# Gate and up projections in seven block products for eight, and the hidden layer in three parts

## The chip, the core and the metric

The kernel runs on one core of one Trainium2 chip. The metric is the device time of one execution in microseconds (us); lower is better. PE is TensorE, DVE VectorE, ACT ScalarE, POOL GpSimd, and SP the engine whose queue issues most transfers.

## What is computed

A trunk of two layers over 512 frames of width 1024. Each layer is a feed-forward block (FFN), an attention mixer, and a second FFN; so there are four FFNs, and they are what the change touches. Everything is float32. Cut to what matters:

```python
def _swiglu(u, w_gate, w_up, w_down):          # w_gate, w_up 1024 x 2816, w_down 2816 x 1024
    return (jax.nn.silu(u @ w_gate) * (u @ w_up)) @ w_down
...
mod = (cond @ ada_w[i] + ada_b[i]).reshape(c.shape[0], N_MOD, D_MODEL)[:, :, None, :]
sh1, sc1, g1, sh2, sc2, g2, sh3, sc3, g3 = [mod[:, j] for j in range(N_MOD)]
u = _rmsnorm(h, norm_g[i, 0]) * (1 + sc1) + sh1
h = h + MACARON_WEIGHT * g1 * _swiglu(u, ffn_w_gate[i, 0], ffn_w_up[i, 0], ffn_w_down[i, 0])
```

After the first FFN comes the mixer with g2, then the second FFN with sh3, sc3 and g3.

## The kernel before

Activations lie transposed: features on the 128 partitions, the 512 frames along the row. A weight chunk of 128x1024 is loaded as `raw` (`wload`), and `wsplit` makes a rounded part `wh` (a copy on ACT) and the rest `wl` (a subtraction on DVE). `mm3` multiplies in three matmuls, wh by the activation's rounded part, wh by its rest, and wl by the rounded part. So every product waits for ACT and then for DVE on its weights, and each matmul loads a 128x128 block and streams the frames past it.

`ffn` makes the 22 tiles of the hidden layer one after the other (`unit`): 24 matmuls of 512 frames for gate into a `pj` bank, 24 for up into an `s` bank, then `gated` (Silu on ACT, product on DVE, split into hid tiles by both). The first tiles of each FFN stand apart, since they run in halves of 256 frames while the norm before them ends, or, in the first FFN, as x arrives. When all 22 are there, `back_proj` makes the eight output tiles (k = 0 to 7) of 66 matmuls each from three weight chunks, and adds each to h (`Back.tile`), the last tile in halves.

The modulation `mod` is the largest other load: 144 chunks of 512 KB (`ada_chunk`), each multiplied with `cond` and summed on DVE. They stand in the list `pending`. `background(n)` issues the next n of them, and each multiply is placed behind the last instruction noted in `mark`, on DVE's queue. `need` issues as many as it takes until a gate's columns are there. All of this runs from in-order queues, one an engine. [...]

## Time and profile before

| | |
|---|---|
| median of 3 runs | 2013.37 us (2010.99 to 2013.88) |
| the profiled execution's own time | 2006.17 us |
| its span, first to last instruction | 2004.4 us |
| PE busy | 1956.1 us, 98% of the span |
| DVE busy | 1094.6 us, 55% |
| ACT busy | 744.7 us, 37% |
| POOL busy | 120.4 us, 6% |

Shares are means over the whole span. The stages follow each other: the start and the first FFN up to about 388 us, the first mixer up to 704, an FFN up to 1070, an FFN up to 1426, the second mixer up to 1626, and the last FFN. A profiled execution and a median of other executions need not agree to the microsecond; here they lie 7.2 us apart.

### The profile page before, as it was taken

How to read it: one execution, taken by the hardware profiler on the slowest of the kernel's cores; microseconds unless marked ns; L12 is line 12 of the kernel's file. 1: busy time of each engine (PE TensorE's matmuls, PEld its weight loads, DVE VectorE, ACT ScalarE, POOL GpSimd, SP SyncE). 2: the span in 40 equal slices, each digit the busy share in tenths (PEclk: the TensorE clock that was granted, in tenths of full speed). 3: DMA queues.
4: the chain of work that ended last, by engine and by line, in shares of the span. 5: the costliest groups of instructions: out<-in, count | busy, mean ns of one | idle time of the engine just before them, and what ended most of it. 6: DMA issues, size and time to landing. Idle time of an engine off the chain costs nothing.

```text
span 2004.4 us, 25366 instructions
## 1 busy us (share of the span) xinstructions
PE 1956.1 (98%) x9988; PEld 1652.8 (82%) x9988; DVE 1094.6 (55%) x1893; ACT 744.7 (37%) x1232; POOL 120.4 (6%) x116
## 2 busy tenths in 40 slices
PE   7999999999989999999999999999999999999997
PEld 4888888987878888888889888888988898888886
DVE  7466673479946577777336433323586573333234
ACT  6322222246667442222224233222357543232221
POOL 0000000045553000000000000000000000000000
PEclk9999999999999999999999999999999999999998
DMA  9467773232222238887432333233232023322331
GB/s 334 135 228 241 236 234 105 92 107 67 85 79 80 85 121 270 280 274 248 117 97 85 107 99 95 92 98 97 71 99 71 23 94 109 103 95 95 95 97 61
DMA packets 78412, 260.53 MB, mean 130 GB/s; under 512 B 9426, under 2 KB 12498, under 8 KB 78292
## 3 DMA queue, kind: packets, MB, share of 16 engines
q1 hardware_dynamic: 75892, 254.65, 39.5%
q0 software_dynamic: 1664, 3.28, 0.7%
q8 instruction: 78, 1.28, 0.3%
q10 hardware_dynamic: 736, 0.98, 0.2%
q14 instruction: 42, 0.34, 0.1%
HBM read 249.17 MB, written 2.10 MB: 125 GB/s over the span
## 4 chain that ended last, share of the span: by engine, by line
PE 83%; DVE 10%; ACT 3%; DMA 2%; issue 1%; POOL 1%; SPq 0%; DVEq 0%; ACTq 0%; POOLq 0%
PE pj L299 18%; PE pj L301 18%; PE pj L300 18%; PE s L301 9%; PE s L300 9%; PE s L299 9%; DVE hid L978 1%; DVE m L977 1%; DVE wl L266 1%; DVE hid L767 1%; DVE hid L350 1%; DVE sm L699 1%; PE aux L718 1%; ACT wide L707 1%; ACT wh L265 1%
## 5 line engine op out<-in xcount | busy, mean ns | idle before, releaser
L265 ACT ACTIVATE wh<-raw 128x1024 fp32r<-128x1024 f32 (+1 forms) x331 | 340.8, 1030 | 899.6 <-PE pj L300 561.9
L266 DVE TENSOR_TENSOR wl<-raw,wh 128x1024 fp32r<-128x1024 f32 (+2 forms) x308 | 364.6, 1184 | 417.5 <-ACT wh L265 417.0
L299 PE MATMUL pj<-u,wh 128*128 128x512 f32 (+1 forms) x1035 | 391.1, 379 | 2.0 <-ACT u L349 0.9
L301 PE MATMUL pj<-u,wl 128*128 128x512 f32 (+1 forms) x1035 | 382.5, 370 | 0.7 <-DVE wl L266 0.5
L300 PE MATMUL pj<-u,wh 128*128 128x512 f32 (+1 forms) x1035 | 381.4, 370 | 0.8 <-DVE u L350 0.8
L299 PE MATMUL pj<-hid,wh 128*128 128x512 f32 (+1 forms) x876 | 319.5, 365 | 0.2 <-DVE h L441 0.2
L300 PE MATMUL pj<-hid,wh 128*128 128x512 f32 (+1 forms) x876 | 317.2, 362 | 0.0
L301 PE MATMUL pj<-hid,wl 128*128 128x512 f32 (+1 forms) x876 | 317.2, 362 | 0.0
L301 PE MATMUL s<-u,wl 128*128 128x512 f32 (+1 forms) x841 | 311.3, 370 | 0.0
L300 PE MATMUL s<-u,wh 128*128 128x512 f32 (+1 forms) x841 | 310.8, 370 | 0.0
L299 PE MATMUL s<-u,wh 128*128 128x512 f32 (+1 forms) x841 | 310.6, 370 | 0.0
L299 PEld LDWEIGHTS pj<-u,wh 128*128 128x128 f32 x1035 | 196.3, 190 | 35.6 <-issue 3.1
L301 PEld LDWEIGHTS pj<-u,wl 128*128 128x128 f32 x1035 | 195.5, 189 | 34.4 <-DVE wl L266 1.5
L300 PEld LDWEIGHTS pj<-u,wh 128*128 128x128 f32 x1035 | 195.6, 189 | 31.2 <-DVE u L350 1.9
L186 DVE SCALAR_TENSOR_TENSOR wide<-wide,cond 128x1024 f32<-128x1024 f32 x133 | 161.3, 1223 | 73.4 <-DMA wide<-in_ada 73.2
L299 PEld LDWEIGHTS pj<-hid,wh 128*128 128x128 f32 x876 | 165.5, 189 | 25.8 <-DVE hid L770 0.4
L301 PEld LDWEIGHTS pj<-hid,wl 128*128 128x128 f32 x876 | 165.3, 189 | 25.4
L300 PEld LDWEIGHTS pj<-hid,wh 128*128 128x128 f32 x876 | 165.4, 189 | 24.9
L301 PEld LDWEIGHTS s<-u,wl 128*128 128x128 f32 x841 | 158.8, 189 | 26.8
L300 PEld LDWEIGHTS s<-u,wh 128*128 128x128 f32 x841 | 158.6, 189 | 26.5
L299 PEld LDWEIGHTS s<-u,wh 128*128 128x128 f32 x841 | 158.5, 189 | 26.0
L557 DVE TENSOR_TENSOR t<-t,s 128x512 f32<-128x512 f32 (+1 forms) x93 | 60.5, 651 | 162.8 <-PE s L301 159.5
(214 smaller groups left out, 1920.2 us busy)
## 6 DMA issues: line engine op xcount, KB each, us to landing
raw<-in_wgu SPq DMA_DIRECT2D x176, 512.0 KB, 3.5
wide<-in_ada SPq DMA_DIRECT2D x133, 512.0 KB, 4.4
raw<-in_wd SPq DMA_DIRECT2D x64, 512.0 KB, 3.5
raw<-in_wd SPq DMA_DIRECT2D x32, 384.0 KB, 3.1
raw<-in_hin SPq DMA_DIRECT2D x19, 512.0 KB, 3.5
h<-in_ada SPq DMA_DIRECT2D x11, 512.0 KB, 7.1
raw<-in_hv SPq DMA_DIRECT2D x8, 512.0 KB, 3.5
raw<-in_hout SPq DMA_DIRECT2D x8, 512.0 KB, 3.6
```

The source lines that it names most:

```text
L186: V.scalar_tensor_tensor(raw, raw, 1.0, cond[0], op0=ALU.mult, op1=ALU.mult, accum_out=mod[l][:, j, k:k + 1])
L265: S.activation(wh[:, :n], raw[:, :n], AF.Copy)
L266: (by or V).tensor_tensor(wl[:, :n], raw[:, :n], wh[:, :n].bitcast(F32), op=ALU.subtract)
L299: PE.matmul(ps, ah, bh, start=start, stop=False)
L300: PE.matmul(ps, ah, bl, start=False, stop=False)
L301: last_mm[0] = PE.matmul(ps, al, bh, start=False, stop=stop).ins
L350: return V.tensor_tensor(ol, raw, oh.bitcast(F32), op=ALU.subtract)
L557: V.tensor_tensor(sg[:, :w], sg[:, :w], pu[:, :w], op=ALU.mult)
L699: V.tensor_reduce(nmx, ps[:, :n], axis=AX.X, op=ALU.max, negate=True)
L707: S.activation(pr[qt], pr[qt], AF.Copy, scale=rinv[:, qt:qt + 1])
L718: last_mm[0] = PE.transpose(ps[:, c:c + P], pr[qt][:, kt * P:(kt + 1) * P], ident).ins
L767: V.tensor_tensor(ol, ps, oh.bitcast(F32), op=ALU.subtract)
```

## The change

**Products.** Two hidden tiles are made at once (`pair`). For gate and for up, the 2x2 blocks of weights (two chunks of 128 inputs by two tiles) and of activations (two chunks by two halves of 256 frames) are multiplied in seven block products (`pair_products`): for each of four pairs of input chunks, seven times three matmuls of 256 frames, into four banks. Three of the seven weight blocks are sums, made by three POOL subtractions in `weight_sums`; ACT and DVE then split 896 columns. The activations' sums are made once an FFN (`input_sums`), by POOL, and split. Four DVE additions put the tiles together from the banks.

**Parts.** The hidden layer is made in three parts of 6, 8 and 8 tiles, and after each part the down projection of that part is added to h for all eight output tiles. The gate's columns g are so wanted after the first part. In the last part three output tiles run in halves, where one did.

**Modulation.** The rate of `background` is one chunk a pair (it was 2 to 4 a tile) and two an output tile in the first two parts. The chunks land in the `raw` buffers, four now for two, which the weights use too, and no longer in the two `wide` ones. `g3` of the first layer is loaded in the second FFN.

The diff, cut to its core:

```diff
-NRAW = 2
+NRAW = 4
...
     def ada_chunk(l, j, k, raw=None):
-        raw = wide_tile()[:, :D] if raw is None else raw
+        raw = raw_tile() if raw is None else raw
...
+    def input_sums(t1, t2):
+        lo, hi = slice(0, HALF), slice(HALF, T)
+        G.tensor_tensor(t1[:, lo], t1[:, hi], t1[:, lo], op=ALU.subtract)
+        G.tensor_tensor(t1[:, hi], t1[:, hi], t2[:, hi], op=ALU.add)
+        G.tensor_tensor(t2[:, hi], t2[:, hi], t1[:, lo], op=ALU.add)
+        G.tensor_tensor(t2[:, lo], t2[:, lo], t2[:, hi], op=ALU.subtract)
...
+    def weight_sums(ap):
+        raw = raw_tile()
+        nc.sync.dma_start(raw[:, :512], ap)
+        r = raw.rearrange("p (s c) -> p s c", s=8)
+        G.tensor_tensor(r[:, 4:6], r[:, 0:1].to_broadcast([P, 2, P]), r[:, 1:4:2], op=ALU.subtract)
+        G.tensor_tensor(r[:, 6], r[:, 3], r[:, 4], op=ALU.subtract)
+        G.tensor_tensor(r[:, 7], r[:, 2], r[:, 6], op=ALU.subtract)
...
+        S.activation(wh[:, :896], raw[:, P:], AF.Copy)
+        V.tensor_tensor(wl[:, :896], raw[:, P:], wh[:, :896].bitcast(F32), op=ALU.subtract)
+        return wh, wl
...
+    def pair_products(src, u, sums):
+        banks[0] += 1
+        b = [pj_ps(), s_ps(), aux_ps(), s_ps() if banks[0] % 2 else aux_ps()]
...
+                mm3(o, wh[:, sl], wl[:, sl], *x, q == 0 and n < 4, q == KD // 2 - 1 and n in (0, 4, 5, 6))
+        r = wide_tile().rearrange("p (s c) -> p s c", s=5)
+        S.activation(r[:, 3], b[0][:, lo], AF.Copy)
...
+        V.tensor_tensor(r[:, 0:5:4], r[:, 3:4].to_broadcast([P, 2, HALF]), two(b[1]), op=ALU.add)
+        V.tensor_tensor(r[:, 1:3], r[:, 4:5].to_broadcast([P, 2, HALF]), two(b[2]), op=ALU.add)
+        V.tensor_tensor(r[:, 3], r[:, 2], b[2][:, lo], op=ALU.add)
+        V.tensor_tensor(r[:, 1:3], r[:, 1:3], two(b[3]), op=ALU.add)
...
+    PARTS = ((0, 6), (6, 14), (14, 22))
...
+        def pair(j):
+            g = pair_products(lambda q: d["wgs"][l, f, j // 2, 0, q], u, sums)
+            S.activation(g, g, AF.Silu)
+            p = pair_products(lambda q: d["wgs"][l, f, j // 2, 1, q], u, sums)
+            V.tensor_tensor(p, p, g, op=ALU.mult)
+            for i in range(2):
+                hidden.append((hid_tile(), hid_tile()))
+                mark[0] = split(*hidden[-1], p[:, i * T:(i + 1) * T]).ins
+            background(rate[0])
...
-        for j in range(j0, NF):
-            unit(j, *load(j), 0, T)
-            background(rate)
...
+        for p0, p1 in PARTS:
+            for j in range(max(j0, p0), p1, 2):
+                pair(j)
...
+            g = gate()
+            if p1 < NF:
+                for k in range(KD):
+                    ps = pj_ps()
+                    run_tile(ps, down(k), act, 0, T)
+                    mark[0] = V.scalar_tensor_tensor(h[:, k], ps, g[:, k:k + 1], h[:, k],
+                                                     op0=ALU.mult, op1=ALU.add).ins
+                    background(rate[1])
+            else:
+                back_proj(g, down, act, nxt, 3)
...
-    pending.extend(ada_work(0, [("g", 0), ("n", 1), ("g", 1), ("n", 2), ("g", 2)]))
+    pending.extend(ada_work(0, [("g", 0), ("n", 1), ("g", 1), ("n", 2)]))
```

In the rows of order below, raw, wh and wl are weights, and `raw<-raw,cond` into mod is a modulation chunk's multiply.

**Place 1, DVE in the down projection of the first FFN.** Before, between two additions to h from pj banks:

```order
L266 TENSOR_TENSOR wl_2347<-raw_2344,wh_2346 128x1024
L366 TENSOR_TENSOR t_2077<-t_2077,t_2251 128x512
L266 TENSOR_TENSOR wl_2353<-raw_2350,wh_2352 128x1024
L266 TENSOR_TENSOR wl_2359<-raw_2356,wh_2358 128x768
L441 SCALAR_TENSOR_TENSOR h<-pj_2254,g_0_997,h 128x512
L266 TENSOR_TENSOR wl_2436<-raw_2433,wh_2435 128x1024
L366 TENSOR_TENSOR t_2077<-t_2077,t_2340 128x512
L266 TENSOR_TENSOR wl_2442<-raw_2439,wh_2441 128x1024
L266 TENSOR_TENSOR wl_2448<-raw_2445,wh_2447 128x768
```

After the change, in the first part's down projection (768 columns are six tiles' weights):

```order
L269 TENSOR_TENSOR wl_977<-raw_974,wh_976 128x768
L269 TENSOR_TENSOR wl_1009<-raw_1006,wh_1008 128x768
L691 SCALAR_TENSOR_TENSOR h<-pj_973,g_0_970,h 128x512
L189 SCALAR_TENSOR_TENSOR raw_999,mod_92<-raw_999,cond_94 128x1024
L189 SCALAR_TENSOR_TENSOR raw_1002,mod_92<-raw_1002,cond_94 128x1024
L691 SCALAR_TENSOR_TENSOR h<-pj_1005,g_0_970,h 128x512
L189 SCALAR_TENSOR_TENSOR raw_1031,mod_92<-raw_1031,cond_94 128x1024
L189 SCALAR_TENSOR_TENSOR raw_1034,mod_92<-raw_1034,cond_94 128x1024
L269 TENSOR_TENSOR wl_1041<-raw_1038,wh_1040 128x768
L269 TENSOR_TENSOR wl_1073<-raw_1070,wh_1072 128x768
L691 SCALAR_TENSOR_TENSOR h<-pj_1037,g_0_970,h 128x512
```

Each addition to h is now followed by two modulation multiplies, and the weights of the next two output tiles stand behind two such groups.

**Place 2, DVE where the first FFN's gate columns g_0 are formed.** Before, in the middle of the hidden tiles:

```order
L350 TENSOR_TENSOR hid_991<-t_987,hid_990 128x512
L186 SCALAR_TENSOR_TENSOR wide_994,mod_92<-wide_994,cond_94 128x1024
L186 SCALAR_TENSOR_TENSOR wide_1000,mod_92<-wide_1000,cond_94 128x1024
L208 TENSOR_TENSOR g_0_997<-mod_92,vec 128x8
L210 TENSOR_SCALAR g_0_997<-g_0_997 128x8
L266 TENSOR_TENSOR wl_1165<-raw_1162,wh_1164 128x1024
L186 SCALAR_TENSOR_TENSOR wide_1003,mod_92<-wide_1003,cond_94 128x1024
L557 TENSOR_TENSOR t_1068<-t_1068,s_1043 128x512
L266 TENSOR_TENSOR wl_1171<-raw_1168,wh_1170 128x1024
```

After the change, between the first part's last pair (its last hid split is the first row) and its down projection:

```order
L353 TENSOR_TENSOR hid_935<-wide_923,hid_934 128x512
L189 SCALAR_TENSOR_TENSOR raw_946,mod_92<-raw_946,cond_94 128x1024
L189 SCALAR_TENSOR_TENSOR raw_949,mod_92<-raw_949,cond_94 128x1024
L189 SCALAR_TENSOR_TENSOR raw_952,mod_92<-raw_952,cond_94 128x1024
L189 SCALAR_TENSOR_TENSOR raw_955,mod_92<-raw_955,cond_94 128x1024
L189 SCALAR_TENSOR_TENSOR raw_958,mod_92<-raw_958,cond_94 128x1024
L189 SCALAR_TENSOR_TENSOR raw_961,mod_92<-raw_961,cond_94 128x1024
L189 SCALAR_TENSOR_TENSOR raw_964,mod_92<-raw_964,cond_94 128x1024
L189 SCALAR_TENSOR_TENSOR raw_967,mod_92<-raw_967,cond_94 128x1024
L211 TENSOR_TENSOR g_0_970<-mod_92,vec 128x8
L213 TENSOR_SCALAR g_0_970<-g_0_970 128x8
L269 TENSOR_TENSOR wl_977<-raw_974,wh_976 128x768
```

The multiplies that stood one to three a tile now stand in one run of eight, ahead of the first weights of the down projection.

**Place 3, DVE among the hidden tiles.** Before, one tile of the first FFN:

```order
L557 TENSOR_TENSOR t_1224<-t_1224,s_1199 128x512
L266 TENSOR_TENSOR wl_1327<-raw_1324,wh_1326 128x1024
L350 TENSOR_TENSOR hid_1228<-t_1224,hid_1227 128x512
L186 SCALAR_TENSOR_TENSOR wide_1231,mod_92<-wide_1231,cond_94 128x1024
L186 SCALAR_TENSOR_TENSOR wide_1234,mod_92<-wide_1234,cond_94 128x1024
L266 TENSOR_TENSOR wl_1404<-raw_1401,wh_1403 128x1024
L186 SCALAR_TENSOR_TENSOR wide_1237,mod_92<-wide_1237,cond_94 128x1024
```

After the change, half of a pair's cycle, from the product of gate and up to the end of the next gate's recombination:

```order
L645 TENSOR_TENSOR wide_1489<-wide_1489,wide_1358 128x1024
L580 TENSOR_TENSOR wl_1648<-raw_1642,wh_1647 128x896
L353 TENSOR_TENSOR hid_1497<-wide_1489,hid_1496 128x512
L580 TENSOR_TENSOR wl_1678<-raw_1672,wh_1677 128x896
L353 TENSOR_TENSOR hid_1501<-wide_1489,hid_1500 128x512
L189 SCALAR_TENSOR_TENSOR raw_1504,mod_92<-raw_1504,cond_94 128x1024
L580 TENSOR_TENSOR wl_1708<-raw_1702,wh_1707 128x896
L609 TENSOR_TENSOR wide_1631<-wide_1631,s_1508 128x2x256
L610 TENSOR_TENSOR wide_1631<-wide_1631,aux_1509 128x512
L580 TENSOR_TENSOR wl_1738<-raw_1732,wh_1737 128x896
L611 TENSOR_TENSOR wide_1631<-wide_1631,aux_1509 128x256
L612 TENSOR_TENSOR wide_1631<-wide_1631,s_1510 128x512
```

The weights' splits are 896 wide, four a product, and four additions that read PSUM banks stand between them.

## Rows read from the trace of the kernel before

**Rows 1.** The page: busy time of each engine, and the chain that ended last.

```profile
PE 1956.1 (98%) x9988; PEld 1652.8 (82%) x9988; DVE 1094.6 (55%) x1893; ACT 744.7 (37%) x1232; POOL 120.4 (6%) x116
...
PE 83%; DVE 10%; ACT 3%; DMA 2%; issue 1%; POOL 1%; SPq 0%; DVEq 0%; ACTq 0%; POOLq 0%
```

**Rows 2.** Windows: a down projection, 18 hidden tiles; columns as its head says.

```profile
core 0: us, PE busy (x) PEld busy (x) DVE busy (x) ACT busy (x) POOL busy (x), PEclk, DMA share, GB/s
...
263.10:388.00 124.90, 124.71 (x611) 105.72 (x610) 60.34 (x95) 31.17 (x38) 1.04 (x2) 1.00 0.44 138
...
1110.40:1306.00 195.60, 195.60 (x865) 161.97 (x864) 74.05 (x84) 58.23 (x76) 0.00 (x0) 1.00 0.31 98
```

**Rows 3.** Timeline of PE (start, duration in us): first and last of 20 matmuls.

```profile
699.93 0.28 PE L300 MATMUL pj<-hid,wh 128*128 128x256 f32 x1
...
702.20 0.28 PE L301 MATMUL pj<-hid,wl 128*128 128x256 f32 x1
```

**Rows 4.** Groups by line and shape on DVE: busy us, mean ns, idle before.

```profile
L266 DVE TENSOR_TENSOR wl<-raw,wh 128x1024 fp32r<-128x1024 f32 x268 | 328.0, 1224 | 306.9 <-ACT wh L265 306.4
L186 DVE SCALAR_TENSOR_TENSOR wide<-wide,cond 128x1024 f32<-128x1024 f32 x133 | 161.3, 1223 | 73.4 <-DMA wide<-in_ada 73.2
...
L557 DVE TENSOR_TENSOR t<-t,s 128x512 f32<-128x512 f32 x81 | 55.5, 686 | 159.5 <-PE s L301 159.5
...
L266 DVE TENSOR_TENSOR wl<-raw,wh 128x768 fp32r<-128x768 f32 x36 | 34.5, 957 | 110.6 <-ACT wh L265 110.6
L441 DVE SCALAR_TENSOR_TENSOR h<-pj,g,h 128x512 f32<-128x512 f32 x34 | 25.5, 750 | 66.6 <-PE pj L301 66.6
...
L186 DVE DVE_READ_ACCUMULATOR wide<-wide,cond 128x1 f32 x133 | 10.9, 82 | 0.0
```

**Rows 5.** Groups by line and shape on ACT.

```profile
L265 ACT ACTIVATE wh<-raw 128x1024 fp32r<-128x1024 f32 x291 | 308.3, 1059 | 769.5 <-PE pj L300 440.6 <-issue 195.1 <-PE s L300 60.6
...
L265 ACT ACTIVATE wh<-raw 128x768 fp32r<-128x768 f32 x36 | 30.5, 846 | 127.9 <-PE pj L300 119.5 <-PE pj L301 3.9 <-DMA raw<-in_wd 2.2
```

**Rows 6.** DMA issues: count, KB each, median us from issue to landing.

```profile
wide<-in_ada SPq DMA_DIRECT2D x133, 512.0 KB, 4.4
...
raw<-in_wd SPq DMA_DIRECT2D x32, 384.0 KB, 3.1
...
raw<-in_uqr SPq DMA_DIRECT2D x4, 192.0 KB, 2.4
```

**Rows 7.** Timeline of PE around a wait in the first mixer.

```profile
423.71 0.38 PE L299 MATMUL pj<-wh,u 128*128 128x256 f32 x1 [0.85 <-ACT wh L265]
426.71 0.39 PE L300 MATMUL pj<-wl,u 128*128 128x256 f32 x1 [2.62 <-POOL wl L266]
...
427.68 0.41 PE L299 MATMUL pj<-wh,u 128*128 128x256 f32 x1
...
430.03 0.41 PE L301 MATMUL pj<-wh,u 128*128 128x256 f32 x1
```

**Rows 8.** Windows around the same wait, columns as in rows 2.

```profile
417.00:427.00 10.00, 6.54 (x38) 5.25 (x37) 9.23 (x9) 3.81 (x6) 6.11 (x4) 1.00 0.57 156
427.00:430.50 3.50, 3.50 (x19) 3.50 (x19) 3.40 (x5) 2.14 (x4) 3.45 (x4) 0.51 0.48 150
```

**Rows 9.** Timeline of POOL, subtractions and products in the first mixer.

```profile
417.79 2.38 POOL L266 TENSOR_TENSOR wl<-raw,wh 128x1024 fp32r<-128x1024 f32 x1
...
609.36 1.28 POOL L658 TENSOR_TENSOR hid<-hid,hid 128x512 f32<-128x512 f32 x1
...
616.66 1.29 POOL L658 TENSOR_TENSOR hid<-hid,hid 128x512 f32<-128x512 f32 x1
```

**Rows 10.** Timeline of DVE at the same times.

```profile
417.47 3.25 DVE L350 TENSOR_TENSOR hid<-hid,hid 64x512 fp32r<-64x512 f32 x1
...
610.28 1.45 DVE L266 TENSOR_TENSOR wl<-raw,wh 128x1024 fp32r<-128x1024 f32 x1 [1.49 <-ACT wh L265]
...
616.80 0.69 DVE L350 TENSOR_TENSOR hid<-aux,hid 128x512 fp32r<-128x512 f32 x1
```

More of the change, by code (lines that the diff above doesn't have):

```diff
@@ L181, with raw_tile @@
     mark = [None]
+    def raw_tile():
+        return wp.tile([P, 1024], F32, tag="raw", name=nm("raw"), bufs=NRAW)
     def ada_chunk(l, j, k, raw=None):
-        raw = wide_tile()[:, :D] if raw is None else raw
+        raw = raw_tile() if raw is None else raw
         nc.sync.dma_start(raw, d["ada"][l, j * KD + k])
@@ L246, in wload @@
     def wload(ap, n):
-        raw = wp.tile([P, 1024], F32, tag="raw", name=nm("raw"), bufs=NRAW)
+        raw = raw_tile()
         nc.sync.dma_start(raw[:, :n], ap)
@@ L540, in first_products @@
             mm3(ps, wh[:, sl], wl[:, sl], *u[k], k == 0, k == KD - 1)
-    def ffn(l, f, u, gate, nxt, feed=None, rate=2, after=None):
+    HALF = T // 2
+    def input_sums(t1, t2):
[4 more added lines that the diff above has]
+        G.tensor_tensor(t2[:, lo], t2[:, lo], t2[:, hi], op=ALU.subtract)
+        out = []
+        for t in (t1, t2):
+            o = hid_tile(), hid_tile()
+            split(*o, t)
+            out += [tuple(x[:, c] for x in o) for c in (lo, hi)]
+        return [out[0], out[3], out[1], out[2]]
@@ new lines, with two @@
+    banks = [0]
+    def pair_products(src, u, sums):
+        banks[0] += 1
+        b = [pj_ps(), s_ps(), aux_ps(), s_ps() if banks[0] % 2 else aux_ps()]
+        lo, hi = slice(0, HALF), slice(HALF, T)
+        for q in range(KD // 2):
+            wh, wl = weight_sums(src(q))
+            b1, b2 = u[2 * q], u[2 * q + 1]
+            t1, t2, t3, t4 = sums[q]
+            for n, (o, w, x) in enumerate((
+                    (b[0][:, lo], 0, [v[:, lo] for v in b1]),
+                    (b[1][:, lo], 1, [v[:, lo] for v in b2]),
+                    (b[2][:, lo], 4, t1),
+                    (b[3][:, lo], 6, [v[:, hi] for v in b2]),
+                    (b[1][:, hi], 5, t2),
+                    (b[2][:, hi], 3, t3),
+                    (b[3][:, hi], 2, t4))):
+                sl = slice(w * P, (w + 1) * P)
+                mm3(o, wh[:, sl], wl[:, sl], *x, q == 0 and n < 4, q == KD // 2 - 1 and n in (0, 4, 5, 6))
+        r = wide_tile().rearrange("p (s c) -> p s c", s=5)
+        S.activation(r[:, 3], b[0][:, lo], AF.Copy)
+        def two(x):
+            return x.rearrange("p (s c) -> p s c", s=2)
+        V.tensor_tensor(r[:, 0:5:4], r[:, 3:4].to_broadcast([P, 2, HALF]), two(b[1]), op=ALU.add)
+        V.tensor_tensor(r[:, 1:3], r[:, 4:5].to_broadcast([P, 2, HALF]), two(b[2]), op=ALU.add)
+        V.tensor_tensor(r[:, 3], r[:, 2], b[2][:, lo], op=ALU.add)
+        V.tensor_tensor(r[:, 1:3], r[:, 1:3], two(b[3]), op=ALU.add)
+        return r.rearrange("p s c -> p (s c)")[:, :2 * T]
@@ L543, in ffn @@
+    PARTS = ((0, 6), (6, 14), (14, 22))
+    def ffn(l, f, u, sums, gate, nxt, feed=None, rate=(2, 2), after=None):
         hidden = []
@@ L577, in ffn @@
                 gated(j, *pss[j], 0, T)
+            unit(j0, *load(j0), 0, T)
+            j0 = 4
         else:
@@ L588, in ffn, with down, u_next @@
                     gated(j, *pss, c0, c1)
-        for j in range(j0, NF):
-            unit(j, *load(j), 0, T)
-            background(rate)
-            if after is not None and j == after[0]:
-                after[1]()
-        def down(k):
-            out = []
-            for c, (k0, k1) in enumerate(((0, 8), (8, 16), (16, 22))):
-                wh, wl = wchunk(d["wd"][l, f, k][:, k0 * P:k1 * P], (k1 - k0) * P)
-                out.append((wh, wl, k1 - k0))
-            return out
-        back_proj(gate(), down, hidden, nxt, 1)
-    def u_next(l, sub):
+        for p0, p1 in PARTS:
+            for j in range(max(j0, p0), p1, 2):
+                pair(j)
+            if after is not None and p1 == NF:
+                after()
+            act = hidden[p0:p1]
+            def down(k):
+                return [(*wchunk(d["wd"][l, f, k][:, p0 * P:p1 * P], (p1 - p0) * P), p1 - p0)]
+            g = gate()
[8 more added lines that the diff above has]
+                back_proj(g, down, act, nxt, 3)
+    def u_next(l, sub, keep=False):
         outs = [(u_tile(), u_tile()) for _ in range(KD)]
+        kept, sums = [], []
         def nxt(acc, c0, c1):
@@ L618, in two @@
                     rb = spread(dg[0], c1 - c0)
-                apply(h_tiles(), rb, c0, c1, acol[l, sub], bcol[l, sub], outs)
+                if keep and not kept:
+                    kept.extend(hid_tile(F32) for _ in range(KD))
+                apply(h_tiles(), rb, c0, c1, acol[l, sub], bcol[l, sub], outs, kept)
+                if keep and c1 == T:
+                    for q in range(KD // 2):
+                        for k in (2 * q, 2 * q + 1):
+                            G.tensor_scalar(kept[k], kept[k], bcol[l, sub][:, k:k + 1], None, op0=ALU.add)
+                        sums.append(input_sums(kept[2 * q], kept[2 * q + 1]))
             later(HOLD1, one)
             later(HOLD2, two)
-        return outs, nxt
+        return (outs, sums), nxt
     def rope_tables(fcol, scol):
@@ L1292, in final @@
                     nc.sync.dma_start(d["out"][:, 4 * g:4 * g + 4, c0:c1], o)
-            ffn(1, 1, u, need(gcol, (1, 2)), final)
+            ffn(1, 1, *x, need(gcol, (1, 2)), final)
 def _consts():
```

46 lines of the change are left out of this document (29 added, 17 removed).

## The prediction

> **What bounds the kernel now.** I read the page first: PE is busy for 98% of the span, and 83% of the chain that ended last is PE's; DVE, at 55%, has 10% of it [rows 1]. The windows say the same stage by stage: through 18 hidden tiles, and in a down projection, PE is busy for practically all of the time [rows 2]. So before, whatever the other engines do is hidden. The change takes work from PE and gives DVE and POOL more, so two questions decide: what PE's part is worth, and where PE must now wait for a queue that had slack.
>
> **Columns.** 18 tiles took 195.6 us [rows 2], 10.87 a tile, 21.73 a pair. In 256-frame form 19 steps from the first to the last of 20 matmuls took 2.27 us [rows 3], 0.1195 each. A pair is now 2 x 84 of them, 20.07. Seven products for eight would be 12.5% less, but the narrow form costs more a column, and 1.66 us a pair (7.6%) is left. There are 39 pairs (9 in the first FFN, where four tiles stand apart, 10 in the others): **-65 us**. Two more output tiles an FFN in halves cost 0.6 us each time, which I put with the small things.
>
> **Down projection with modulation chunks.** Place 1 of the order is the largest term. Per output tile DVE has an addition to h, 0.75, and two chunk multiplies of 1.223 + 0.082 [rows 4]. An addition waits for PE's last matmul of its tile, and the multiplies are placed behind it, so none can run ahead. The weights of tiles 2 and 3 stand behind the second group. So PE ends tile 1, and only then DVE does an addition (0.75), two multiplies (2.61) and the first split (0.96 for 768 columns) [rows 4]: 4.3, with gaps 4.5; PE, which has no other work in its row, waits. With 1024 columns the split is 1.22, the wait 4.7. I checked that it is not the load: that chunk can be issued when the first group's first multiply has freed a buffer, 2.05 us after tile 0's end; 3.1 landing [rows 6], 0.85 on ACT [rows 5] and the split make 7.0, and the queue gets there at 8.6 (one tile of 18 matmuls is 4.1). This comes three times a part, and a fourth time before the next part's first product. The order shows it in five parts: two each in the first and second FFN, the first in the third. 5 x 4 x 4.6 = **+92**. It could be nothing only if the multiplies left the queue between; the order excludes that.
>
> **The clock.** Before, PE had been idle for most of 3 us when, just after it took up work at 426.71, the 256-frame matmuls took 11 steps in 2.35 us, 0.214 each [rows 7], and the granted clock of that stretch was 0.51, the lower of the two levels (1.2 of 2.4 GHz), after 1.00 [rows 8]. Some 17 matmuls at 0.094 more are 1.6 us lost. The 20 waits above are longer than that one. Bounds 0 and 1.7 a wait; I take the row it is nearest to, 1.6: **+32**.
>
> **The gate after the first part.** Place 2. PE needs the hid splits of the last pair and the first down weights. From the last product's end: a copy on ACT and hand-overs 0.55, four additions (three at 0.69; one of 256 columns at about 0.42, by the splits' slope of 1.04 ns a column) 2.5 [rows 4], the product of 1024 columns 1.22, two splits 2.1: 6.5. Then eight multiplies follow. Four buffers are full: 5.2, until 11.7. Each of the others waits for a buffer from the multiply four before it and for a landing, 4.4 by the chunks' row [rows 6]: the last ends at about 17.3. The down weights take a buffer of the fifth, 3.1 and 0.85 more, and split at 18.3. PE idles for all of it. The second FFN has seven multiplies there: 17.3. **+36**, and 3 for the clock, which goes into the small things. In the third FFN the gate is there long before.
>
> **The other ends of parts** would cost 6.5 minus six tiles (4.1) each, but PE's row lets tile 1 begin in between: 0.3 to 1.5 each, some 10. The second FFN's last part has three chunks after an addition, ahead of tile 1's weights: 6, and two waits of 2: 10. **+20.**
>
> **Inside the pairs.** Per pair DVE has eight splits of 896 columns (between 0.957 and 1.224 [rows 4]: 1.09), eight additions (5.0), a product (1.22), two hid splits (1.37), gaps (0.6): 16.9, and 18.2 with a chunk; PE's 20.07 covers it. POOL's forms are not in the trace; from 1.28 at 512 columns and 2.38 at 1024 [rows 9], 256 is 0.73 and 128 is 0.46: 1.65 a weight block, 13.2 a pair, which is covered too. But the two are not independent. At 417 a DVE split of two SBUF operands lasted 3.25 for 0.69 and ended when POOL's subtraction did and half a microsecond more; at 610 one of 1024 columns lasted 1.45 for 1.22, again behind POOL; at 616.8 a split that reads PSUM (aux) lasted 0.69 right through POOL's work [rows 9, 10]. So each split, product and chunk multiply can wait for the POOL instruction that runs, up to 0.73, and the additions from PSUM do not. A chunk also holds one of four `raw` buffers over its pair, and a weight block then waits for the third before it: landing some 2.6 (between 2.4 for 192 KB and 3.1 for 384 [rows 6]), POOL 1.65, ACT 0.95, DVE 1.09 and hand-overs, 6.8. Closed around DVE's row (third place), that is 20.4 a pair without any wait for POOL. With nine DVE instructions on this loop, each waiting 0.17 on average, and POOL's own waits, 22.3: 2.2 over PE. Bounds: 0 (all waits covered), and 5.7 (every such DVE instruction and every POOL one apart: 12.6 + 13.2 = 25.8 minus 20.07). I take 2.2, nearer the low end since POOL's instructions are short: 17 pairs, **+37**. The 22 pairs without a chunk have four buffers and 3.2 us of DVE slack: 0.3 each, **+7**; uncovered it would be 4.4.
>
> The Trainium skill, SBUF — State Buffer, section Who interferes with whom, says that a DVE instruction with two SBUF inputs contends with a GpSimd instruction that reads SBUF, as an exclusive lock for the whole instruction. The three places above agree with it; taken as if both engines always met, it gives the upper bound, the second rival.
>
> **Small things**: input sums on POOL and DVE at each FFN's start (at most three us each, mostly ahead of need), halves, the clock at the gate's two waits. **+8.**
>
> **Sum.** -65 + 92 + 32 + 36 + 20 + 37 + 7 + 8 = +167. On the profiled execution's 2006.2 that is 2173; the median lies 7.2 above that execution, so 2180.
>
> **Rivals.**
> *Cheap waits.* POOL and DVE interleave without loss, and PE is back at full clock at once: without 37, 7 and 32 the sum is +91: 2104. For it: POOL's instructions are short, and DVE has slack on average. Against: a row that shows the clock fall after a shorter wait.
> *The port is the bound.* DVE's and POOL's instructions exclude each other throughout: 17 x 5.7 + 22 x 4.4 = 194 in place of 44: 2330. For it: the long waits at 417. Against: at 610 the split behind POOL took 0.14 less than alone, and the additions from PSUM leave POOL room.
> *Not slower.* The chunk multiplies cost PE nothing, because DVE gets to the weights behind them before PE needs them, as it did before. All of the large terms are waits behind such multiplies: 92, their clock 32, the gate's 36, 10 at the second FFN's last part and 37 in the pairs, 207 together; without them 1973. It decides at a fifth of that: below 40 in all the kernel is not slower, which is a wait of about 1.2 us, clock and all, where I have 6.2. For it: DVE is busy for 55% only, and 133 such multiplies cost PE nothing before. Against: a queue in the order printed cannot pass an addition that waits for PE.
> *The change does nothing to PE*: if the narrow matmuls took half of 0.227 they would give 2.7 a pair, and if 0.13 nothing; the twenty steps speak against both.
>
> **How the numbers follow.** Forecast (2140 to 2230) 0.62; cheap waits (2085 to 2140) 0.15; port (2230 to 2350) 0.16; not slower 0.07, of it 0.03 within 0.2% of 2013 (what a measurement of this kernel can tell from no change) and 0.04 faster. The range leaves the ends of the two outer cases out: 2090 to 2270. Slower 0.93.
>
> **What would show it.** PE's busy share falls from 98% to about 88%. A pair without a chunk takes 20.1 to 20.5 between its Silus, one with a chunk about 22. In the first FFN's first down projection PE shows waits of some 4.5 us for wl at every second output tile, and one of about 18 ahead of it, with the clock at the lower level after them. Weight splits of 896 columns last over 1.09 on average. It is wrong if those waits are not there, or if the pairs take 24 and more.

## The result and the profile after

The changed kernel takes **2271.07 us** (median of 4 runs, 2266.89 to 2274.52), the kernel before 2013.62 beside it: **1.128** times as long, with an interval of 1.1258 to 1.1302. The forecast was 2180, in a range of 2090 to 2270. The direction was right, the size 91 us too small, and the time lies just above the range. The profiled execution took 2274.52 us over a span of 2272.7; against the 2006.2 of before that is +268, which is what the parts below are summed to (the medians lie 257 apart).

The page, busy time of each engine and the chain that ended last, as in [rows 1]:

```profile
PE 2010.7 (88%) x12820; PEld 1794.3 (79%) x12820; DVE 1565.1 (69%) x2434; ACT 917.6 (40%) x1467; POOL 1023.1 (45%) x1140
...
PE 41%; POOL 22%; DVE 19%; DMA 6%; issue 6%; ACT 5%; POOLq 0%; DVEq 0%; SPq 0%; ACTq 0%
```

PE's share fell to 88%, as forecast, and more than half of the chain is no longer PE's; of the others POOL has most, 22%. What PE waited for, in us, times and the longest:

```profile
PE pj L302 <- ACT wh L268: 73.9, 25, 17.3
PE pj L304 <- DVE wl L580: 40.6, 67, 1.1
PE pj L302 <- ACT wh L579: 31.0, 8, 6.8
PE pj L302 <- ACT hid L352: 25.1, 10, 3.6
PE pj L304 <- DVE wl L269: 22.2, 22, 2.3
```

L268 and L269 are the down projections' weights, L579 and L580 the pairs', L352 the hidden tiles. The windows tell the stages apart. They run from the first matmul of one stage to that of the next, so the wait at a stage's end lies in it. In order: the first FFN's first down projection, four pairs, second down projection, four pairs; the starts of the second (the wait for its gate in it) and third FFN up to their first down projection; in the third FFN four pairs, down projection, four pairs; the start of the fourth, and four of its pairs.

```profile
core 0: us, PE busy (x) PEld busy (x) DVE busy (x) ACT busy (x) POOL busy (x), PEclk, DMA share, GB/s
117.94:174.12 56.18, 40.91 (x145) 30.26 (x145) 32.27 (x50) 6.87 (x8) 4.32 (x5) 0.86 0.63 205
174.12:265.20 91.08, 85.57 (x673) 83.50 (x673) 69.30 (x78) 40.14 (x50) 80.44 (x92) 0.97 0.42 121
265.20:340.08 74.88, 55.69 (x194) 41.92 (x192) 38.93 (x58) 9.50 (x10) 3.71 (x4) 0.84 0.49 158
340.08:435.50 95.42, 86.38 (x672) 82.89 (x673) 68.86 (x78) 40.09 (x50) 80.60 (x95) 0.98 0.42 120
817.87:904.58 86.71, 62.59 (x465) 60.92 (x463) 62.31 (x88) 31.85 (x50) 59.11 (x60) 0.85 0.31 99
1294.79:1367.44 72.65, 59.96 (x457) 57.72 (x456) 56.05 (x74) 32.22 (x50) 62.27 (x63) 0.93 0.28 79
1428.66:1517.75 89.09, 83.38 (x672) 81.26 (x673) 67.40 (x77) 40.15 (x50) 79.59 (x93) 1.00 0.38 108
1517.75:1566.11 48.36, 45.47 (x194) 37.03 (x193) 22.69 (x24) 11.01 (x13) 12.81 (x19) 0.96 0.28 85
1566.11:1646.74 80.63, 80.63 (x673) 80.63 (x672) 61.36 (x69) 39.73 (x50) 68.00 (x78) 1.00 0.41 110
1899.60:1968.26 68.66, 59.81 (x457) 57.95 (x456) 47.09 (x64) 30.40 (x48) 60.89 (x63) 0.95 0.26 70
2003.59:2084.22 80.63, 80.63 (x673) 80.63 (x672) 62.31 (x69) 39.18 (x49) 67.75 (x78) 1.00 0.39 111
```

A stage's loss is its length less its matmuls at their best step, the time from the start of one to the start of the next: 0.1200 for 256 frames (80.63 over 672) and 0.2264 for 512 (195.6 over 864, [rows 2]). The first down projection needs 144 x 0.2264 = 32.6 and took 56.2. Two rows are worth comparing: at 1428.66 and at 1566.11 stand four pairs each, in the same FFN and without a chunk inside, and the first four take 8.5 us longer. Ahead of them lies a down projection with chunks, ahead of the others one without; and POOL has 93 instructions in the one window and 78 in the other.

Place 1 of the order, DVE in the first down projection (start, duration, what it does, idle before):

```profile
122.67 0.96 DVE L269 TENSOR_TENSOR wl<-raw,wh 128x768 fp32r<-128x768 f32 x1 [3.79 <-ACT wh L268]
123.89 0.75 DVE L691 SCALAR_TENSOR_TENSOR h<-pj,g,h 128x512 f32<-128x512 f32 x1 [0.26 <-PE pj L304]
124.55 1.22 DVE L189 SCALAR_TENSOR_TENSOR raw<-raw,cond 128x1024 f32<-128x1024 f32 x1
...
127.97 0.75 DVE L691 SCALAR_TENSOR_TENSOR h<-pj,g,h 128x512 f32<-128x512 f32 x1 [1.04 <-PE pj L304]
128.63 1.21 DVE L189 SCALAR_TENSOR_TENSOR raw<-raw,cond 128x1024 f32<-128x1024 f32 x1
...
129.78 1.22 DVE L189 SCALAR_TENSOR_TENSOR raw<-raw,cond 128x1024 f32<-128x1024 f32 x1
...
130.92 0.95 DVE L269 TENSOR_TENSOR wl<-raw,wh 128x768 fp32r<-128x768 f32 x1
```

PE ended its second tile by 127.9; addition, two multiplies and the split followed one another, and PE's first use of that wl is at 131.93, 4.0 us later, of which two matmuls with wh filled the smaller part. This is the wait that the prediction put at 4.3, with gaps 4.5: its pieces are right, its length a little less.

POOL and DVE among the pairs, groups by shape (instructions, busy us, mean ns):

```profile
L576 POOL TENSOR_TENSOR raw<-raw 128x128 f32<-128x128 f32 x312 | 305.4, 979 | 24.5
L574 POOL TENSOR_TENSOR raw<-raw 128x256 f32<-128x256 f32 x312 | 276.5, 886 | 903.8 <-DMA raw<-in_wgs 768.9 <-DVE h L691 82.0 <-DVE hid L416 24.7
L575 POOL TENSOR_TENSOR raw<-raw 128x128 f32<-128x128 f32 x312 | 228.5, 732 | 24.5
...
L719 POOL TENSOR_SCALAR hid<-hid,b 128x512 f32<-128x512 f32 x24 | 44.6, 1860 | 3.2 <-DVE u L421 3.2
```

These are the three subtractions of `weight_sums`; they make four of the seven weight blocks, not three, since the first, with 256 columns, makes two. One call costs POOL 0.98 + 0.89 + 0.73 = 2.60 us and not the 1.65 of the prediction: 20.8 for the eight of a pair, where PE's part is 20.16. And L719, the shift of the inputs, which the prediction did not price apart, takes 1.86.

### The profile page after: what moved, and what is told of

Its sections match the earlier page's. It is cut to its first block, busy times and chain, and to the rows that moved or that the text cites. A ratio compares the mean times of both kernels' runs of the same rounds, so it can differ in the third digit from the quotient of the medians.

```text
span 2272.7 us, 34261 instructions
## 1 busy us (share of the span) xinstructions
PE 2010.7 (88%) x12820; PEld 1794.3 (79%) x12820; DVE 1565.1 (69%) x2434; ACT 917.6 (40%) x1467; POOL 1023.1 (45%) x1140
## 4 chain that ended last, share of the span: by engine, by line
PE 41%; POOL 22%; DVE 19%; DMA 6%; issue 6%; ACT 5%; POOLq 0%; DVEq 0%; SPq 0%; ACTq 0%
PE pj L304 9%; PE pj L302 9%; PE pj L303 9%; POOL raw L576 7%; POOL raw L574 6%; POOL raw L575 5%; DMA raw<-in_wgs 3%; DVE raw L189 3%; DVE wl L269 2%; PE s L302 2%; PE s L303 2%; PE s L304 2%; DMA raw<-in_wd 2%; DVE wl L580 2%; POOL hid L719 2%
## 5 line engine op out<-in xcount | busy, mean ns | idle before, releaser
L574 POOL TENSOR_TENSOR raw<-raw 128x256 f32<-128x256 f32 x312 | 276.5, 886 | 903.8 <-DMA raw<-in_wgs 768.9
L580 DVE TENSOR_TENSOR wl<-raw,wh 128x896 fp32r<-128x896 f32 x312 | 381.8, 1224 | 180.6 <-ACT wh L579 163.2
L579 ACT ACTIVATE wh<-raw 128x896 fp32r<-128x896 f32 x312 | 297.1, 953 | 499.7 <-POOL raw L576 335.8
L268 ACT ACTIVATE wh<-raw 128x1024 fp32r<-128x1024 f32 (+2 forms) x175 | 174.3, 1000 | 403.9 <-DMA raw<-in_wd 251.8
L576 POOL TENSOR_TENSOR raw<-raw 128x128 f32<-128x128 f32 x312 | 305.4, 979 | 24.5
L302 PE MATMUL pj<-u,wh 128*128 128x256 f32 (+1 forms) x723 | 242.4, 336 | 43.0 <-ACT wh L579 31.0
L304 PE MATMUL pj<-u,wl 128*128 128x256 f32 (+1 forms) x723 | 238.7, 330 | 41.1 <-DVE wl L580 40.6
L269 DVE TENSOR_TENSOR wl<-raw,wh 128x1024 fp32r<-128x1024 f32 (+2 forms) x152 | 174.1, 1150 | 121.4 <-ACT wh L268 120.7
L575 POOL TENSOR_TENSOR raw<-raw 128x128 f32<-128x128 f32 x312 | 228.5, 732 | 24.5
L303 PE MATMUL pj<-u,wh 128*128 128x256 f32 (+1 forms) x723 | 231.6, 321 | 3.8 <-DVE u L353 2.7
L303 PE MATMUL aux<-hid,wh 128*128 128x256 f32 x780 | 222.4, 285 | 0.0
L302 PE MATMUL aux<-hid,wh 128*128 128x256 f32 x780 | 222.4, 285 | 0.0
L304 PE MATMUL aux<-hid,wl 128*128 128x256 f32 x780 | 222.3, 285 | 0.0
L302 PE MATMUL s<-u,wh 128*128 128x256 f32 (+1 forms) x685 | 204.1, 298 | 0.0
L303 PE MATMUL s<-u,wh 128*128 128x256 f32 (+1 forms) x685 | 203.6, 297 | 0.0
L304 PE MATMUL s<-u,wl 128*128 128x256 f32 (+1 forms) x685 | 203.5, 297 | 0.0
```

What stands on the lines that cost most here:

```text
L268: S.activation(wh[:, :n], raw[:, :n], AF.Copy)
L269: (by or V).tensor_tensor(wl[:, :n], raw[:, :n], wh[:, :n].bitcast(F32), op=ALU.subtract)
L302: PE.matmul(ps, ah, bh, start=start, stop=False)
L303: PE.matmul(ps, ah, bl, start=False, stop=False)
L304: last_mm[0] = PE.matmul(ps, al, bh, start=False, stop=stop).ins
L574: G.tensor_tensor(r[:, 4:6], r[:, 0:1].to_broadcast([P, 2, P]), r[:, 1:4:2], op=ALU.subtract)
```

## Experiments

Where no interval is given, a kernel was measured once. Two theories at first. *The queue*: PE waits for weights that stand behind chunk multiplies on DVE, and for sums that hold up ACT. *The port*: POOL's sums and DVE's splits hold each other up, chunk or not.

**No chunks.**

```diff
-        raw = raw_tile() if raw is None else raw
+        if raw is None:
+            G.memset(mod[l][:, j, k:k + 1], 0.02)
+            return
```

> Left out: after the first sixteen, every modulation chunk (its load and its multiply on DVE); its column of mod is set to a constant by POOL. In the changed kernel's trace PE's steps above their best (0.1197 us for 256 frames, 0.2265 for 512) sum to 139 us in the five down projections that carry chunks, 34 in the two waits for the gate, 58 in the parts whose pairs carry a chunk, and some 15 in the last parts. The theory of the queue (all of it stands behind chunk multiplies on DVE) expects these to go: 2271 - 245 = about 2025, with 20.2 us a pair throughout and no wait of over 2 us in a down projection. The theory of the port (POOL's weight sums and DVE's splits shut each other out, chunk or not) expects the 58 to stay: about 2083. If parts as such cost the waits (weights only one tile ahead), the 139 stay as well: over 2200.

Measured 2037.9. Four pairs in the first FFN:

```profile
134.20:214.90 80.70, 80.70 (x674) 80.69 (x673) 61.34 (x71) 38.30 (x48) 68.45 (x78) 1.00 0.37 108
```

All parts with four pairs took this. So 233 of the 262 us hang on the chunks, nearly as the theory of the queue had it (2025 expected), and the port by itself makes none of these pairs longer for PE. The other side: with every cost of the chunks gone the change is still 29 us slower than before.

**Weights two tiles ahead.**

```diff
+                ahead = [down(0), down(1)]
                 for k in range(KD):
                     ps = pj_ps()
-                    run_tile(ps, down(k), act, 0, T)
+                    if k + 2 < KD:
+                        ahead.append(down(k + 2))
+                    run_tile(ps, ahead[k], act, 0, T)
```

> The weights of output tile k+2 are asked for ahead of tile k's addition and chunks, so that their splits stand ahead of those multiplies on DVE's queue; nothing is left out. The theory of the queue expects the 139 us lost in the five down projections with chunks to fall to about 15 (DVE has 0.75 + 2.61 + 0.96 = 4.3 us a tile of six against PE's 4.1, and 4.6 against 5.4 with eight): 2271 - 125 = about 2146, and the granted clock stays at 1.00 there. The rival that DVE's amount of work or the four raw buffers set the pace there expects half the loss to stay: about 2200. If the order has nothing to do with it: 2271.

Measured 2189.39, 1.0897 (1.0872 to 1.0922): 82 back, of 125 expected. So the order is a cause, but the time is nearer to the rival's 2200, in which the work and the buffers hold half of the loss. In the first down projection no wait is left between the tiles; one of 7.1 us stands at its end, for the next product's first weights. The middle of that stage, and its end:

```profile
130.00:140.00 10.00, 10.00 (x46) 8.29 (x45) 8.43 (x13) 1.69 (x2) 0.00 (x0) 1.00 0.92 298
150.00:162.00 12.00, 4.87 (x22) 3.75 (x21) 8.79 (x16) 0.95 (x1) 3.23 (x6) 0.85 0.80 268
```

In the middle PE is busy throughout at the full clock, and now the transfers are nearly full: share 0.92 at 298 GB/s. Sixteen chunks of 512 KB and eight weight chunks of 384 are 11.5 MB, for which 32.6 us of PE's work would ask 353 GB/s. Of the chain of work between 125 and 165 us 55% are transfers and 24% DVE, so the transfers are the larger part of it; that they alone set the pace is not shown.

**The parts alone, with the products of before.**

```diff
         def pair(j):
+            for i in (j, j + 1):
+                unit(i, *load(i), 0, T)
+            background(rate[0])
+            return
```

> Only the parts: the pairs are made as two tiles one after the other in 24 + 24 matmuls of 512 frames, as before the change, with one chunk for every two tiles; parts, chunks and the input sums (not used) stay. The theory of the queue expects the down projections' 139 and the gates' 34 to stay, the pairs to take 21.73 each with the chunk hidden (39 x (21.73 - 20.16) = +61, less the 58 lost in pairs with a chunk), and the 50 lost where the FFNs start (PE waits for POOL's input sums) to go: 2271 + 61 - 58 - 50 = about 2225. The theory of the port (what POOL does is the cause of the loss) expects most of the 240 to go with POOL's sums: under 2100.

Measured 2197.26, 28 less than expected. Parts and chunks alone make 188 of the 262 us, without one POOL sum of weights; the seven products, with all their sums, do not earn their 61 but cost 74 more. The five down projections lost 101 here, not 140: the waits between their tiles are the same, those in the first tile for the last hidden tiles and at the end for the next product's weights are shorter (3.4 for 5.9 us in the first).

**A chunk's multiply cut short in the pairs, and five buffers.** The first covers 64 of 1024 columns of a multiply in a pair; the second is

```diff
-NRAW = 4
+NRAW = 5
-                   dynamic_dma_scratch_size=8192)
+                   dynamic_dma_scratch_size=4096)
```

> Cut: the multiply of a chunk that lies in a pair covers 64 of its 1024 columns; its load, its buffer and its place in DVE's queue stay. The down projections' chunks stay whole. If DVE's time makes the pairs with a chunk long (1.3 us more a pair on an engine that the port slows), they fall from 23.2 to about 20.4 us: 16 x 2.8 = 45 less, about 2226. If it is the raw buffer that the chunk holds until it has landed (a weight block then waits for the third before it), they stay over 22: about 2255 to 2271.

> Five raw buffers in place of four (the room comes from halving the scratch of POOL's own DMA queue); nothing left out. The theory of the held buffer (a chunk keeps one of four raw buffers until it has landed and its place in DVE's queue has come, so that a weight block waits for the third before it) expects the 16 pairs with a chunk to fall from about 23.1 us to about 20.5: 2271 - 42 = about 2229, with the waits in the down projections as they were (ninth and tenth chunk of the gate's run start earlier: 3 us at each gate less at most). If DVE's time or the port sets those pairs, they stay at 23: 2265 to 2271.

Measured 2263.09 and 2194.07 (1.0908, 1.0886 to 1.093). The same four pairs of the first FFN in the one and the other:

```profile
175.70:265.20 89.50, 85.55 (x672) 83.65 (x673) 65.06 (x78) 40.04 (x50) 77.95 (x92) 0.97 0.42 126
```

```profile
165.70:257.80 92.10, 83.80 (x672) 81.37 (x673) 72.78 (x84) 39.78 (x49) 82.72 (x93) 1.00 0.43 128
```

Neither shortens the pairs much (91.08 in the changed kernel). The held buffer was my explanation in the prediction, and as the main cause it falls. The 77 us of the fifth buffer came from the down projections, where the weights could be asked for earlier (the first took 48.5 for 56.2): a gain, for a reason that I had not given.

**Late sums.** ACT adds the shift, and its copies of the sums are queued behind the norm's last activation, two edits that this run does not part:

```diff
-                            G.tensor_scalar(kept[k], kept[k], bcol[l, sub][:, k:k + 1], None, op0=ALU.add)
-                        sums.append(input_sums(kept[2 * q], kept[2 * q + 1]))
+                            S.activation(kept[k], kept[k], AF.Identity, bias=bcol[l, sub][:, k:k + 1])
+                        sums.append(input_sums(kept[2 * q], kept[2 * q + 1], last_u[0]))
```

> At the start of the second to fourth FFN the shift b is added to the kept input by ACT and no longer by POOL (eight instructions of 1.6 to 2.9 us each), and ACT's copies that split the sums are queued behind the norm's last activation; nothing left out. The trace of the changed kernel shows ACT waiting 3.6, 3.7, 3.0 us for POOL's sums with the norm's activations, the Silus and weight copies queued behind, and PE loses 16, 20 and 16 us at these starts where it lost about 1 before. The theory that this queue is the cause expects some 10 to 13 back at each: 2271 - 35 = about 2236. If PE waits there because the norm itself ends late (three output tiles in halves, POOL's port), less than a third comes back: over 2260.

Measured 2238.16 (1.1135, 1.1106 to 1.1164), as expected. What was mended, in the changed kernel at the fourth FFN's start, on ACT and on POOL:

```profile
1902.75 0.51 ACT L420 ACTIVATE u<-hid,b 128x256 fp32r<-128x256 f32 x1 [0.27 <-DVE hid L416]
1906.85 0.63 ACT L352 ACTIVATE hid<-hid 128x512 fp32r<-128x512 f32 x1 [3.59 <-POOL hid L560]
1907.39 1.29 ACT L420 ACTIVATE u<-hid,b 128x256 fp32r<-128x256 f32 x3
```

```profile
1901.76 3.56 POOL L719 TENSOR_SCALAR hid<-hid,b 128x512 f32<-128x512 f32 x2 [0.45 <-DVE u L421]
1905.30 0.72 POOL L559 TENSOR_TENSOR hid<-hid 128x256 f32<-128x256 f32 x1
1906.10 0.72 POOL L560 TENSOR_TENSOR hid<-hid,hid 128x256 f32<-128x256 f32 x1
```

ACT takes up a copy of the sums, waits 3.59 us for POOL, and the norm's own `u`, which the FFN's first tiles need, stands behind it. The longest wait of PE at these starts, 6.8 us up to 1326.12 in the third FFN, is for a pair's weights, and their copy stood behind the last copies of sums in the same way:

```profile
1324.60 0.63 ACT L352 ACTIVATE hid<-hid 128x512 fp32r<-128x512 f32 x1 [1.50 <-POOL hid L562]
1325.14 0.93 ACT L579 ACTIVATE wh<-raw 128x896 fp32r<-128x896 f32 x1
```

In the three starts PE waited 7.0 us for `u` and 11.8 for these copies; with late sums for both together under 0.5. Some 28 of the 33 us came back in these three stages, which took 76.80, 63.40 and 58.90.

**Filled waits.**

```diff
+                    if pending and k and k % 2 == 0:
+                        with tc.issue_after(last_mm[0]):
+                            for _ in range(16):
+                                m = PE.matmul(spare_ps, act[0][0][:, :P], act[1][0], start=True, stop=True).ins
```

> Added: in the five down projections with chunks, ahead of output tiles 2, 4 and 6, sixteen matmuls of 512 frames into an unused bank (3.6 us at the full clock), in the place of PE's wait of 4.2 to 4.6 us; the result is not used. The theory that the lower clock is the price of each wait expects PE to stay at the level of 1.00 there and 15 of the 25 steps down to the lower level to go: of the 47 us by which the matmuls in these stages are slow, some 28, so about 2243. If the clock falls for another cause, nothing changes or the added matmuls delay what waits: 2271 or more.

Measured 2276.46. The first down projection, as in the first row of the windows above:

```profile
119.50:176.20 56.70, 48.88 (x192) 36.91 (x192) 32.30 (x50) 6.86 (x8) 4.21 (x5) 0.92 0.63 203
```

The granted clock rose from 0.86 to 0.92 (in the stretches from 130 to 170 it was 1.00), and the stage took 56.7 for 56.2. The time lost at the lower clock did not come back: PE, now faster over one tile, waited about 1 us for the next one's weights, and the added matmuls filled the rest. This does not price the clock where nothing else is late.

**No POOL sums.** In `weight_sums` a second load of `ap` into `raw[:, 512:]` stands for the three subtractions.

> Left out: POOL's three subtractions for each weight block; a second load of 192 KB fills the places of the three sums, so the seven products are of other blocks than they should be. After the runs with five buffers and with short multiplies, neither the held buffer nor DVE's time is what makes the pairs with a chunk long. The theory of the port, narrowed (POOL's row is nearly full in a pair, its instructions are lengthened to 2.6 us a block by DVE's, and a chunk's multiply on top makes the weights late) expects these pairs at 20.2 us: 58 less in four parts and a half, and some 10 at the FFNs' starts, about 2205. If the chunk's load or its place on DVE's queue is the cause, POOL or no POOL, they stay at 22.5 and more: about 2260.

Measured 2169.39, 102 less than the changed kernel where 66 were expected. (The second load is 256 KB, not 192, into the places of four sums.) The first FFN's four pairs, and four of the last FFN:

```profile
174.66:256.87 82.21, 82.20 (x672) 82.05 (x673) 62.79 (x81) 39.83 (x50) 0.00 (x0) 0.98 0.76 245
...
1901.90:1982.50 80.60, 80.60 (x673) 80.60 (x672) 59.30 (x71) 40.16 (x50) 0.00 (x0) 1.00 0.66 204
```

It is POOL's sums: the first of the parts behind chunks falls from 91.08 to 82.21, the next from 95.42 to 84.40, and the third FFN's from 89.09 to 84.30, so that some 4 us stay in these two. This run takes POOL's work away whole; that POOL and DVE lengthen each other is seen in DVE's splits, first in the changed kernel, then in this one:

```profile
L580 DVE TENSOR_TENSOR wl<-raw,wh 128x896 fp32r<-128x896 f32 x312 | 381.8, 1224 | 180.6 <-ACT wh L579 163.2 <-PE s L304 11.1 <-PE aux L304 4.6
```

```profile
L577 DVE TENSOR_TENSOR wl<-raw,wh 128x896 fp32r<-128x896 f32 x312 | 341.3, 1096 | 134.2 <-ACT wh L576 129.4 <-PE s L303 1.2 <-PE aux L304 0.7
```

How a part without chunks escapes it, the Silus of four pairs tell (there is one a pair; first and last start), first in the changed kernel's last FFN, then in this one's:

```profile
L643 ACT ACTIVATE wide<-wide x4: 1046/1062/1062, 2017.2 to 2081.9; 128x1024 f32<-128x1024 f32 x4
```

```profile
L640 ACT ACTIVATE wide<-wide x4: 1043/1044/1047, 1915.4 to 1976.0; 128x1024 f32<-128x1024 f32 x4
```

64.7 over three steps is 21.6 a pair; without POOL 20.2. So while PE runs its pairs in 20.16, the engines beside it need 21.6, nearly the 21.73 of before. Two of the parts in which PE does lose time, in the changed kernel at 1428.66 without a chunk inside, and at 174.12 with one a pair:

```profile
L643 ACT ACTIVATE wide<-wide x4: 1042/1046/1061, 1450.7 to 1516.3; 128x1024 f32<-128x1024 f32 x4
```

```profile
L643 ACT ACTIVATE wide<-wide x4: 1042/1044/1062, 194.1 to 263.8; 128x1024 f32<-128x1024 f32 x4
```

That is 21.9 and 23.2 a pair. So the first runs at much the same period and lacks only a lead; in the second a chunk adds 1.4. PE can be faster for a part, if it has a lead, that is, weights finished ahead of need: in the last FFN and at 1566.11 POOL has summed six of its 32 weight blocks (19 instructions in the row at 1517.75) during the down projection ahead. Chunks in that down projection leave room for little more than one (five instructions in the row at 117.94). This is what parts the rows at 1428.66 and 1566.11 and makes 8.5 of the 10 to 15 us that the parts with chunks inside lose; neither a short multiply nor a buffer gives the lead back. How a chunk adds its 1.4 is open, since neither of these took it away by itself.

**Versions that draw on this.** The last FFN alone in pairs, in two parts, the others as before; then the last two; then these with more for PE to do at the joints and two tiles of each FFN made singly ahead of its pairs.

> A version made from both kernels, nothing left out: the first three FFNs as before the change (22 tiles one after the other, one down projection, chunks at 3 and 4 a tile in the wide buffers); only the last FFN, in which no chunk is left, in pairs, in two parts of 10 and 12 tiles, with the input sums as in the run with late sums, weights two tiles ahead and five raw buffers. If the change loses only by what stands in the queues (chunks, sums) and the products are worth 1.66 us a pair, it takes 10 x 1.66 = 17 off and pays 6 at the start and 2 at the ends: 2010 - 9 = about 2001. If the port makes the pairs cost what the products save, or the start costs 16 as in the changed kernel: 2010 to 2015.

> The same for the last two FFNs, nothing left out; so that the third FFN's input sums find room, the second FFN (products as before, chunks at 4 a tile) is made in two parts of 14 and 8 tiles, with weights two tiles ahead in its first down projection and 2 chunks an output tile there. An output tile of 14 hidden tiles takes PE 9.5 us, DVE 5.5 and two chunks' loads some 6.5, so the queue theory expects nothing lost there: 2010 - 33 + 12 + 6 + 3 = about 1998. If a part with chunks costs PE something whatever the order, the second FFN loses 10 to 25 and the sum is 2005 to 2020.

> From the run with the last two FFNs, nothing left out, two edits: in a part's down projection the first two output tiles are multiplied over all but the last two hidden tiles before either is finished (so PE has work while the last pair is recombined and split), and in the last two FFNs tiles 2 and 3 are made singly, as before the change, ahead of the pairs (so POOL's input sums have 21 us more). From the profile of that run: 7 us lost in the second FFN's first down projection, 10 and 6 at the starts of the third and fourth, 2 to 4 at the end of each first part. The queue theory expects 4.5 + 7 + 4.5 + 5 back, less 2 x 1.66 for two pairs made singly: 2009 - 18 = about 1991. If POOL and DVE hold up PE at these places whatever stands in front, less than 5 comes back: 2004 and more.

The third against the second, cut:

```diff
+                for i in range(2):
+                    seq(run_tile, pss[i], ahead[i], act, 0, T, 0, n)
...
-                    ps = pj_ps()
-                    run_tile(ps, ahead[k], act, 0, T)
+                    ps = pss[k] if k < 2 else pj_ps()
+                    seq(run_tile, ps, ahead[k], act, 0, T, n if k < 2 else 0)
```

Measured 2006.05 (0.9988, 0.9979 to 0.9996), 2009.02 (0.9989, 0.9977 to 1.0001) and **1996.61 (0.9941, 0.9927 to 0.9955)**. They lie 5, 11 and 6 above the theory of the queue, the second within its rival's range. The last beats both kernels, by 0.6%, small but beyond its interval, and by 12%. The six pairs of its last part, in a row:

```profile
1788.60:1911.40 122.80, 121.48 (x1010) 121.04 (x1010) 94.79 (x106) 58.48 (x74) 108.45 (x124) 1.00 0.37 104
```

121.0 would be six at 20.16: a loss of 1.8.

**All four FFNs with every repair.**

> The change in all four FFNs with every repair, nothing left out: five raw buffers, sums late with the shift on ACT, weights two tiles ahead, the next part's first two weight blocks asked for ahead of the last chunks, the first two output tiles begun before the last pair is split, no chunk in a pair (one a pair in the first FFN), two an output tile, three or one in the last part. Summed from the changed kernel's profile: 71 back in the first FFN, 102 in the second, 37 in the third, 18 in the fourth, and some 15 from the tiles begun early: 2271 - 243 = about 2028. If the repairs act on the same time, or the chunks (now all in the down projections, 1.4 MB for each 4.1 us of PE's work against 0.3 MB a us that the run with weights two ahead moved) set the pace there, 2060 to 2120. Under 2009 if the change can win in all four.

Measured 2091.75 (1.0408, 1.0387 to 1.043), the rival's case. Two rows show why, both of parts whose pairs carry no chunk of their own, in the second FFN behind a down projection with chunks (four of its multiplies are left over into the first 9 us) and in the fourth:

```profile
859.70:952.60 92.90, 85.97 (x673) 83.81 (x674) 70.81 (x82) 40.18 (x50) 81.54 (x93) 0.96 0.42 122
...
1824.80:1905.40 80.60, 80.60 (x673) 80.58 (x672) 62.47 (x69) 39.84 (x50) 65.89 (x75) 1.00 0.41 116
```

My sum took every loss in the pairs for the chunks' in them. Moved into the down projections, the chunks took the lead away instead.

## Why the prediction fell short

By its own steps, in us of the profiled execution (measured: lengths of stages less their matmuls at best steps; the last row above the sum is what is left over):

| step | forecast | measured |
|---|---|---|
| columns | -65 | -61 |
| five down projections with chunks, and the clock | 92 + 32 | 140 |
| gates after first parts | 36 | 34 |
| parts of pairs with chunks in them or ahead | 37 | 58 |
| pairs without | 7 | 0 |
| other ends of parts | 20 | 35 |
| small things; measured, the last three FFNs' starts alone | 8 | 47 |
| first FFN's start, mixers | 0 | 15 |
| sum | +167 | +268 |

**Right.** Columns: 39 pairs at 21.73 less 20.16. The gates: waits of 17.3 and 16.6 before the first weights, forecast 18.3 and 17.3. The down projections: the order of DVE's rows, the pieces, the places; the run with weights two tiles ahead moved them, and the run without chunks took them away. Of the 140, 93 are waits (from one matmul's start to the next, less the best step), nearly the sum of 20 x 4.6. That they meet so well is in part luck, since they lie otherwise: mostly 3 to 4 at every second tile, 2 to 6 at a part's end, the rest for hidden tiles and weights in the first two tiles of a part. 47, for 32, is matmuls that took longer without a wait, at a granted clock of 0.81 to 0.86 in these stages. That the clock can be added to the waits at all is not shown: filled waits brought nothing back.

**Failed: the small things.** The term "input sums on POOL and DVE at each FFN's start (at most three us each, mostly ahead of need)" is the largest miss. The three starts lost 14.7 + 18.3 + 14.3 = 47: 86.71 less the gate's 16.6 and 462 x 0.12; 72.65 and 68.66 less 453 x 0.12. The sums were priced by POOL's own time, and who is queued behind them was not asked: ACT's copies of them stood ahead of the norm's activations and of the pairs' first weights. Late sums brought 33 us, some 28 of them here, as that theory had it; the other 19 of the 47 are not explained.

**Failed: how the pairs lose.** The size was 37 for 58, but the reason was wrong. The buffer that a chunk holds is not it (five buffers: 92.1). The prediction closed the loop around a DVE row and gave POOL 1.65 a call; POOL takes 2.60, with its subtractions of 128 columns at 0.73 and 0.98 where the shortest take 0.46, and its eight calls fill 20.8 of a pair. The sign that it named, 20.1 to 20.5 between the Silus of pairs without a chunk, did not come: they lie 21.4 to 21.9 apart. Weights come at that pace, and PE's 20.16 lasts as long as the lead does, which the prediction did not have. The Trainium skill's rule (SBUF — State Buffer, Who interferes with whom: an exclusive lock on the ports that DVE and GpSimd share) agrees with the run without POOL sums, where the mean of the 896-column splits, 1224 ns, fell to 1096; that a lock is the reason these runs do not show. Taken for whole instructions it gave 25.8 for a pair with a chunk, and 23.2 to 24.3 was measured: the two engines' work overlaps in part. The rival built on it missed in the other place, a loss of 4.4 for chunkless pairs, which for PE was 0.

**Failed: the ends.** 20 for 35. A spent lead is paid at the part's end: PE waits 0.5 to 3.6 us there for the last pair's hidden tiles (25.1 us at L352 over ten places, of which three, 10.5 us, lie in the 140), also where no chunk is near. Of the 35, some 15 are the second FFN's last part, forecast 10, where weights stand behind chunk multiplies, as it said.

The 15 at the first start and in the mixers are the remainder and were not looked into.

## What to carry to other kernels

When work moves to an idle engine, price the queue of whoever takes its result, not only the engine: here ACT stood still for POOL's sums with the norm behind it. An engine that is 84% busy beside a busy PE, as POOL is here (67.75 of 80.63), can look free because it works ahead; compare the period of the last step in its chain with PE's, and ask what fills the lead. Cheap background loads are cheap only where engines, buffers and transfers have slack at once: the change pays where none are left, in the last two FFNs, and there only mended.
